# Output projection of a hybrid decoder block: 512 moving columns, left half along k, right half from ya's tiles, another last chain, stores on two queues

## The chip, the core and the metric

The kernel runs on one core of one Trainium2 chip. TensorE (PE) does matmuls into PSUM and loads its stationary operand separately (PEld); VectorE (DVE) and ScalarE (ACT) do elementwise work and are the two that read PSUM here; GpSimd (POOL) works on SBUF alone; SyncE (SP) issues DMAs. Every engine takes its instructions in order, and engines wait for each other by semaphores. The metric is the device time of one execution in microseconds; lower is better. The time shown for the kernel before is the median of 3 runs.

## What is computed

One layer of a decoder block with two parallel branches, an mLSTM (matrix memory) and a native sparse attention, over 512 tokens of width 1024 in float32. What matters here is how the layer ends:

```python
ya = jax.nn.sigmoid(p["m_o"]) * mh * jax.nn.silu(p["m_z"])
...
yb = yn * jax.nn.silu(p["n_z"])
merged = (jax.nn.sigmoid(p["g_a"]) * (ya @ w_branch_a[l])
          + jax.nn.sigmoid(p["g_b"]) * (yb @ w_branch_b[l]))
x = x + merged @ w_out[l]
...
return _rmsnorm(x, final_norm_g)
```

`_rmsnorm` multiplies each row by the inverse root of the mean of its squares plus 1e-6, and by a gain per column. `merged` is 512 x 1024, `w_out` 1024 x 1024.

## The kernel before

**Precision.** Every large product is done in three passes. Each float32 operand is split into a high part (rounded to the type that TensorE takes at full rate, float32r) and a low part, the rest; the product is high x high + high x low + low x high, all three summed in one PSUM bank. `split` (line 129) makes the two: ACT copies the raw tile to the high tile, VectorE subtracts the high from the raw to get the low. `mm3` (line 156) runs the three passes over a list of k blocks of 128 rows; the order is a·c, a·d, b·c with a, b the stationary high and low and c, d the moving ones. `passes` (line 199) is the same as a generator, for work that is fed in small steps.

**Weights.** `weights` (line 140) loads a raw tile of 128 x 1024 values (512 KB) on SP's queue into one of three buffers `wr`, and splits it into `wh` and `wl`, of which there are three each. A raw buffer is free once VectorE has subtracted; a high or low buffer once TensorE has read it for the last time. `wwide` (line 152) makes two such calls, for k blocks 0 to 3 and 4 to 7 of 256 columns.

**Order.** The Python text issues the work in one order; the framework places each engine's instructions by its own estimate of when they can run, and ACT and VectorE keep the order so placed. So a split may stand ahead of work that the text issued earlier. A stream (line 164) runs the projections and the branch products two loads ahead.

**The stages before the change.** The last jobs of the stream are, for j = 0 to 7 (`branch`, line 1030): 128 columns of the gates, of ya @ w_branch_a (24 matmuls of 512 moving columns on `yah` and `yal`, the split ya, [128, 8, 512] each) and of yb @ w_branch_b (12 matmuls on `ybh` and `ybl`). VectorE combines the two with the gates in tiles `s`, and the sum is split into `meh[:, j]` and `mel[:, j]`: merged, transposed, with its 1024 columns as 8 blocks of 128 partitions and the 512 tokens in the free dimension. After the stream, SP's queue loads x into `xo` [128, 4, 1024] and the gain into `fg`, and ACT loads the table that has Ln and Exp.

**The output projection (line 1088 on).** Four column groups `cc` of 256. Each loads its weights by `wwide` and runs over the four row blocks `tb` of 128 tokens: 24 matmuls with `meh` / `mel` stationary and 256 weight columns moving, into one of three banks `pp`. Behind each such block, VectorE adds half of the bank to x (the factor of the gates' sigmoid, which is done by tanh, leaves a 2), ACT squares the result with a running sum into `fs[:, tb, cc]`, and VectorE multiplies by the gain, in place. After the third group VectorE adds up the first three sums of squares and makes `fb` = sum/1024 + eps of them.

**The last chain (`scale_out`, line 1071).** When the fourth sum of a row block is there, ACT does Ln and Exp for a first value r of the inverse root (`fr`), VectorE forms v = last sum/1024 + `fb` (`fv`) and improves r by one Newton step (r·v·r, then 1.5 - half of it, times r). Then VectorE scales columns 0 to 511 and ACT 512 to 1023, and SP issues one store of 256 KB for each half.

Of the kernel before, what the change touches and what calls it, by code (L numbers as in the profile page):

```python
# [11 lines left out]
F32 = mybir.dt.float32  # L12
F32R = mybir.dt.float32r
I32 = mybir.dt.int32
AF = mybir.ActivationFunctionType
OP = mybir.AluOpType
AX = mybir.AxisListType.X

T = 512
D = 1024  # L20
NT = T // 128
ND = D // 128
EPS = 1e-6
# [40 lines left out]
def build(  # L64
# [4 lines left out]
    nc = tc.nc  # L69
# [17 lines left out]
    pe, pool = nc.tensor, nc.gpsimd  # L87
    act, dve = Engine(nc.scalar, "act"), Engine(nc.vector, "dve")
    A = act.activation

    pers = ctx.enter_context(tc.tile_pool(name="pers", bufs=1))
    wp = ctx.enter_context(tc.tile_pool(name="wp", bufs=2))
    psum = ctx.enter_context(tc.tile_pool(name="psum", bufs=2, space=bass.MemoryType.PSUM))

    def bank(tag, bufs):
        return psum.tile([128, 512], F32, name=tag, tag=tag, bufs=bufs)

    PP = lambda: bank("pp", 3)
    PS = lambda: bank("ps", 2)
    PT = lambda: bank("pt", 2)  # L100
    PO = lambda: bank("po", 1)

    def f(ap):
        return ap.bitcast(F32)
# [11 lines left out]
    mhalf = pers.tile([128, 4], F32, name="mhalf")  # L116
    pool.memset(mhalf, -0.5)

    def rsqrt(pl, v, n, tag):
        r = pl.tile([128, n], F32, name=tag + "r", tag=tag + "r")  # L120
        t = pl.tile([128, n], F32, name=tag + "t", tag=tag + "t")
        pool.tensor_tensor(r, v, mhalf[:, :n], OP.pow)
        dve.tensor_tensor(t, v, r, OP.mult)
        dve.tensor_tensor(t, t, r, OP.mult)
        dve.tensor_scalar(t, t, -0.5, 1.5, OP.mult, OP.add)
        dve.tensor_tensor(r, r, t, OP.mult)
        return r

    def split(src, hi, lo, eng="a"):
        if eng == "a":  # L130
            A(hi, src, AF.Copy)
        elif eng == "p":
            pool.tensor_scalar(hi, src, 1.0, 1.0, OP.mult, OP.mult)
        else:
            dve.tensor_copy(hi, src)
        dve.tensor_tensor(lo, src, f(hi), OP.subtract)
# [3 lines left out]
    def weights(src, eng="a"):  # L140
        nk, n = src.shape[1], src.shape[2]
        raw = wp.tile([128, nk, n], F32, name="wr", tag="wr", bufs=3)
        nc.sync.dma_start(raw, src)
        hi = wp.tile([128, nk, n], F32R, name="wh", tag="wh", bufs=3)
        lo = wp.tile([128, nk, n], F32R, name="wl", tag="wl", bufs=3)
        split(raw, hi, lo, eng)
        return hi, lo
# [4 lines left out]
    def wwide(view, c0):  # L152
        ws = [weights(view[:, k : k + 4, c0 : c0 + 256]) for k in (0, 4)]
        return (lambda k: ws[k // 4][0][:, k % 4, :]), (lambda k: ws[k // 4][1][:, k % 4, :])

    def mm3(ps, lh, ll, rh, rl, ks, start=True, stop=True):
        n = len(ks)
        for i, k in enumerate(ks):
            a, b, c, d = lh(k), ll(k), rh(k), rl(k)
            pe.matmul(ps, a, c, start=start and i == 0, stop=False)  # L160
            pe.matmul(ps, a, d, start=False, stop=False)  # L161
            pe.matmul(ps, b, c, start=False, stop=stop and i == n - 1)  # L162
# [86 lines left out]
    with tc.tile_pool(name="ph0", bufs=2, side="right") as p0, tc.tile_pool(  # L249
        name="small", bufs=1, side="right"  # L250
# [3 lines left out]
        raw = sp.tile([128, ND, SW], F32, name="sraw")  # L254
# [6 lines left out]
        for k in (0, 4):  # L261
            ks = slice(k, k + 4)
# [10 lines left out]
        for hf in range(2):  # L273
            ps = PS()
# [68 lines left out]
        last = None  # L343
        for tb in range(NT):
            ts = slice(tb * 128, (tb + 1) * 128)
            for hf in range(2):
                ks = slice(hf * 4, hf * 4 + 4)
# [9 lines left out]
            last = PP()  # L357
# [13 lines left out]
        rows = sp.tile([11, D], F32, name="rows")  # L371
# [11 lines left out]
        ps = PT()  # L383
# [25 lines left out]
        c1 = np.float32(6.28125)  # L409
# [265 lines left out]
    for src, dst in ((cpad, Ct), (spad, St)):  # L675
        ps = PT()
# [205 lines left out]
    yah = yap.tile([128, ND, T], F32R, name="yah")  # L882
    yal = yap.tile([128, ND, T], F32R, name="yal")
# [58 lines left out]
    for h in range(4):  # L942
# [11 lines left out]
        for sb in range(NT):  # L954
            o, n = KOFF[sb], 512 - sb * 128
            bias = cs[:, sb, h : h + 1]
# [5 lines left out]
        for sb in range(NT):  # L962
            o, n = KOFF[sb], 512 - sb * 128
# [33 lines left out]
        r = rsqrt(mp, va, NT, "rl")  # L997
# [26 lines left out]
    with tc.tile_pool(name="fin", bufs=1) as fp:  # L1024
        meh = fp.tile([128, ND, T], F32R, name="meh")
        mel = fp.tile([128, ND, T], F32R, name="mel")
        wav = w_branch_a[0].rearrange("(k p) c -> p k c", p=128)
        wbv = w_branch_b[0].rearrange("(k p) c -> p k c", p=128)
        wov = w_out[0].rearrange("(k p) c -> p k c", p=128)
        def branch(base, j, yh, yl, nk):  # L1030
            def gen(w):
                o = 0 if nk == ND else (j % 2) * 128
                ps = PP()
                yield from passes(
                    ps, lambda k: w[0][:, k, o : o + 128], lambda k: w[1][:, k, o : o + 128],
                    lambda k: yh[:, k], lambda k: yl[:, k], nk,
                )
                s = halves[base, j]
                dve.scalar_tensor_tensor(s, s, 1.0, ps, OP.add, OP.mult)
                if base == GB:  # L1040
                    t = halves.pop((GA, j))
                    dve.tensor_tensor(t, t, halves.pop((GB, j)), OP.add)
                    split(t, meh[:, j], mel[:, j])

            def load():
                if nk == ND:
                    return weights(wav[:, :, j * 128 : j * 128 + 128])
                if j % 2 == 0:
                    halves["w"] = weights(wbv[:, :, j * 128 : j * 128 + 256])
                return halves["w"]  # L1050

            stream.add(load, gen)

        for j in range(ND):
            for base in (GA, GB):
                if (base, j) in later[3:]:
                    gate_ab(base, j, sgp)
            branch(GA, j, yah, yal, ND)
            branch(GB, j, ybh, ybl, 4)
        stream.drain()  # L1060
        xo = fp.tile([128, NT, D], F32, name="xo")
        nc.sync.dma_start(xo, x[0].rearrange("(b p) c -> p b c", p=128))
        fg = fp.tile([128, D], F32, name="fg")
        nc.sync.dma_start(fg, final_norm_g.partition_broadcast(128))
        tc.keep_in_program_order(act.preload_act_table_set("natural_log_exp_and_others"))
        fs = fp.tile([128, NT, 4], F32, name="fs")
        fb = fp.tile([128, NT], F32, name="fb")
        fv = fp.tile([128, NT], F32, name="fv")
        fr = fp.tile([128, NT], F32, name="fr")

        def scale_out(tb):
            part, v, r = fb[:, tb : tb + 1], fv[:, tb : tb + 1], fr[:, tb : tb + 1]
            last = fs[:, tb, 3:4]
            A(r, last, AF.Ln, bias=part, scale=1.0 / D)
            dve.scalar_tensor_tensor(v, last, 1.0 / D, part, OP.mult, OP.add)
            A(r, r, AF.Exp, scale=-0.5)
            dve.scalar_tensor_tensor(v, r, v, r, OP.mult, OP.mult)
            dve.tensor_scalar(v, v, -0.5, 1.5, OP.mult, OP.add)
            dve.tensor_tensor(r, r, v, OP.mult)
            for hf in range(2):  # L1080
                hs = slice(hf * 512, hf * 512 + 512)
                if hf:
                    A(xo[:, tb, hs], xo[:, tb, hs], AF.Copy, scale=r)
                else:
                    dve.tensor_scalar(xo[:, tb, hs], xo[:, tb, hs], r, None, OP.mult)
                nc.sync.dma_start(out[0, tb * 128 : (tb + 1) * 128, hs], xo[:, tb, hs])

        for cc in range(4):
            wh, wl = wwide(wov, cc * 256)
            cs_ = slice(cc * 256, cc * 256 + 256)  # L1090
            for tb in range(NT):
                ps = PP()
                ts = slice(tb * 128, tb * 128 + 128)
                mm3(
                    ps[:, :256], lambda k: meh[:, k, ts], lambda k: mel[:, k, ts],
                    wh, wl, range(ND),
                )
                xv = xo[:, tb, cs_]
                dve.scalar_tensor_tensor(xv, ps[:, :256], 0.5, xv, OP.mult, OP.add)
                jk = fp.tile([128, 256], F32, name="jk", tag="jk", bufs=2)  # L1100
                A(jk, xv, AF.Square, accum_out=fs[:, tb, cc : cc + 1])
                dve.tensor_tensor(xv, xv, fg[:, cs_], OP.mult)
                if cc == 2:
                    v = fb[:, tb : tb + 1]
                    dve.tensor_reduce(v, fs[:, tb, 0:3], AX, OP.add)
                    dve.tensor_scalar(v, v, 1.0 / D, EPS, OP.mult, OP.add)
                if cc == 3:
                    scale_out(tb)


_INS = (
# [19 lines left out]
```

## Time and profile before

| | us |
|---|---|
| median of 3 runs | 645.48 (644.75 to 646.33) |
| the profiled execution, its own time | 644.24 |
| its span, first to last instruction | 642.4 |
| w_out stage: first matmul to last VectorE read of a bank | 589.55 to 635.97 |
| last matmul's read to the end of the span | 635.97 to 642.4 |

The granted clock of TensorE was 0.998 of full speed over the span. Times inside the span count from its first instruction. In a row of the timeline stand the start, the duration, the engine, the line (L80 is the wrapper through which all ACT and VectorE instructions are recorded, so these are told apart by their tiles), the operation, and output <- inputs with partitions x elements; in square brackets the engine's idle time before it and what ended it. A matmul's duration (0.28 or 0.39) includes its way through the array, and they overlap; the distance between their starts is the pitch. SPq is SP's DMA queue: its rows are the issues, not the transfers.

The costliest groups of the whole span, of which the w_out stage has the last three of TensorE:

```profile
L202 PE MATMUL pp<-hTh,wh 128*128 128x512 f32 (+1 forms) x488 | 192.2, 394 | 0.0
...
L161 PE MATMUL pp<-wl,meh 128*128 128x256 f32 x128 | 36.2, 283 | 0.0
L160 PE MATMUL pp<-wh,meh 128*128 128x256 f32 x128 | 36.2, 283 | 0.0
L162 PE MATMUL pp<-wh,mel 128*128 128x256 f32 x128 | 36.2, 284 | 0.0
```

### The profile page before, as it was taken

Reading aid. Unit: us, or ns where it says so; the run is one execution under the profiler, and the core shown is the slowest. Engines: PE = TensorE matmul, PEld = TensorE weight load, DVE = VectorE, ACT = ScalarE, POOL = GpSimd, SP = SyncE. Lnnn points to the kernel's source line nnn. Section 1 sums busy time; section 2 is a strip of 40 time slices with the busy share of each in tenths; the row PEclk is TensorE's granted clock in tenths of the full one; section 3 lists DMA queues with packets and bytes.
Section 4 is the critical chain, followed back from the end, with each engine's and each line's share of the span. In section 5 each row is a group of like instructions: output and inputs, shape, how many; then the busy total and the mean of one; then the engine's idle time right before and its main releaser. Section 6 shows DMA issues by size and latency. Waiting matters only on the chain.

```text
span 642.4 us, 9274 instructions
## 1 busy us (share of the span) xinstructions
PE 626.9 (98%) x3470; PEld 538.8 (84%) x3470; DVE 411.5 (64%) x878; ACT 302.4 (47%) x604; POOL 54.0 (8%) x114
## 2 busy tenths in 40 slices
PE   6999999999999999999999999999999999999995
PEld 4988788888878788888989889889888888888995
DVE  5796768767866865557669788696554233334455
ACT  5653554655655655435545546545322222223234
POOL 5000021121121231100000000000000000000000
PEclk9999999999999999999999999999999999999999
DMA  8476421122122212223313222232274242423203
GB/s 248 136 193 154 120 66 45 55 67 67 36 64 66 65 49 83 66 70 96 99 37 96 80 73 78 67 78 87 66 232 128 66 131 67 128 70 108 90 1 131
DMA packets 90124, 58.74 MB, mean 91 GB/s; under 512 B 4016, under 2 KB 86100, under 8 KB 90080
## 3 DMA queue, kind: packets, MB, share of 16 engines
q1 hardware_dynamic: 90080, 58.16, 31.8%
q8 instruction: 27, 0.44, 0.3%
q14 instruction: 17, 0.14, 0.1%
HBM read 55.01 MB, written 2.10 MB: 89 GB/s over the span
## 4 chain that ended last, share of the span: by engine, by line
PE 88%; DVE 7%; ACT 2%; DMA 1%; issue 1%; SPq 0%; POOL 0%; DVEq 0%; POOLq 0%
PE pp L204 21%; PE pp L202 21%; PE pp L206 21%; PE pp L162 3%; PE pp L160 3%; PE pp L161 3%; PE pt L784 2%; DVE wl L80 2%; PE po L797 1%; PE ps L769 1%; PE po L796 1%; PE ps L537 1%; ACT wh L80 1%; PE ps L770 1%; PE ps L162 1%
## 5 line engine op out<-in xcount | busy, mean ns | idle before, releaser
L202 PE MATMUL pp<-hTh,wh 128*128 128x512 f32 (+1 forms) x488 | 192.2, 394 | 0.0
L204 PE MATMUL pp<-hTl,wh 128*128 128x512 f32 (+1 forms) x488 | 191.3, 392 | 0.0
L206 PE MATMUL pp<-hTh,wl 128*128 128x512 f32 (+1 forms) x488 | 191.1, 392 | 0.0
L80 DVE TENSOR_TENSOR wl<-wr,wh 128x1024 fp32r<-128x1024 f32 x88 | 109.0, 1240 | 74.3 <-ACT wh L80 73.9
L80 ACT ACTIVATE wh<-wr 128x1024 fp32r<-128x1024 f32 x88 | 92.9, 1057 | 114.3 <-PE pp L204 82.8
L206 PEld LDWEIGHTS pp<-hTh,wl 128*128 128x128 f32 x488 | 91.8, 188 | 16.2
L202 PEld LDWEIGHTS pp<-hTh,wh 128*128 128x128 f32 x488 | 92.0, 188 | 15.3
L204 PEld LDWEIGHTS pp<-hTl,wh 128*128 128x128 f32 x488 | 92.0, 189 | 15.1
L778 POOL TENSOR_SCALAR P<-P,st 128x128 f32<-128x128 f32 (+1 forms) x64 | 38.5, 620 | 182.2 <-DVE st L80 134.1
L80 ACT ACTIVATE P<-P,st 128x128 f32<-128x128 f32 (+3 forms) x64 | 35.7, 558 | 36.6 <-DVE st L80 36.4
L80 DVE CUSTOM_DVE_ANT_0 P<-ps,cst 128x128 f32<-128x128 f32 (+3 forms) x64 | 30.4, 486 | 22.0 <-PE ps L770 21.6
L80 ACT ACTIVATE pth<-pt 128x512 fp32r<-128x512 f32 (+1 forms) x64 | 27.2, 434 | 29.8 <-PE pt L784 18.6
L80 DVE TENSOR_TENSOR ptl<-pt,pth 128x512 fp32r<-128x512 f32 (+1 forms) x64 | 30.4, 484 | 16.4 <-ACT pth L80 15.7
L204 PE MATMUL pp<-wl,hTh 128*128 128x256 f32 x128 | 36.2, 283 | 0.0
L206 PE MATMUL pp<-wh,hTl 128*128 128x256 f32 x128 | 36.2, 283 | 0.0
L202 PE MATMUL pp<-wh,hTh 128*128 128x256 f32 x128 | 36.2, 283 | 0.0
L161 PE MATMUL pp<-wl,meh 128*128 128x256 f32 x128 | 36.2, 283 | 0.0
L160 PE MATMUL pp<-wh,meh 128*128 128x256 f32 x128 | 36.2, 283 | 0.0
L162 PE MATMUL pp<-wh,mel 128*128 128x256 f32 x128 | 36.2, 284 | 0.0
L80 DVE SCALAR_TENSOR_TENSOR u<-pp,prm,u 128x511 f32<-128x511 f32 (+2 forms) x48 | 35.6, 742 | 0.4
L80 DVE SCALAR_TENSOR_TENSOR s<-s,pp 128x512 f32<-128x512 f32 x16 | 11.0, 687 | 29.5 <-PE pp L206 29.5
L784 PE MATMUL pt<-cst,P 128*128 128x128 f32 x160 | 28.6, 274 | 0.3 <-DVE ptl L80 0.3
(272 smaller groups left out, 1112.0 us busy)
## 6 DMA issues: line engine op xcount, KB each, us to landing
wr<-w_in SPq DMA_DIRECT2D x68, 512.0 KB, 3.9
wr<-w_branch_a SPq DMA_DIRECT2D x8, 512.0 KB, 3.8
wr<-w_out SPq DMA_DIRECT2D x8, 512.0 KB, 3.5
wr<-w_branch_b SPq DMA_DIRECT2D x4, 512.0 KB, 3.6
xo<-x SPq DMA_DIRECT2D x1, 2048.0 KB
out<-xo SPq DMA_DIRECT2D x8, 256.0 KB, 2.2
xt<-x SPq DMA_DIRECT2D x3, 512.0 KB, 5.8
k<-k SPq DMA_DIRECT2D x8, 128.0 KB, 2.3
```

The source lines that it names most:

```text
L80: ins = fn(*args, **kw)
L160: pe.matmul(ps, a, c, start=start and i == 0, stop=False)
L161: pe.matmul(ps, a, d, start=False, stop=False)
L162: pe.matmul(ps, b, c, start=False, stop=stop and i == n - 1)
L202: pe.matmul(ps, a, c, start=k == 0, stop=False)
L204: pe.matmul(ps, a, d, start=False, stop=False)
L206: pe.matmul(ps, b, c, start=False, stop=k == nk - 1)
L537: pe.matmul(ph[:, :64], W1[i][:, j, :], Xs[i][:, j].rearrange("p g n -> p (g n)"), start=j == 0, stop=j == 15,)
L769: pe.matmul(pss[:, :n], tq, kh[:, b, :n], start=True, stop=False)
L770: pe.matmul(pss[:, :n], tq, kl[:, b, :n], start=False, stop=True)
L778: pool.tensor_scalar(pj, pj, st[:, 2, j : j + 1], 1.0, OP.mult, OP.mult)
L784: pe.transpose(pt[:, (qb - kb) * 128 : (qb - kb) * 128 + 128], P[:, POFF[qb] + kb * 128 : POFF[qb] + kb * 128 + 128], ident,)
```

## The change

**Left half.** The columns 0 to 511 of the output are computed along k: four banks (two of `ps`, two of `pt`, which the stages before use and this one did not), one for each row block, stay open while four weight pairs of two k blocks and 512 columns each go by. A pair serves 4 x 6 matmuls of 512 moving columns.

**Right half.** The raw weights of columns 512 to 1023 are loaded in between, two k blocks at a time, on SP's queue into the same three `wr` buffers, and split into `yah` and `yal`, which branch A has read by then. There they stay, so each row block runs its 24 matmuls at once, 512 columns wide into a `pp` bank; the last row block is cut into two pieces of 256 columns.

**Pieces.** `piece` does the addition, the square and the gain on 512 columns at a time (256 for the last two). For the very last one the addition goes to a tile of its own, `xg`, so that the gain's product and ACT's Square both read it. `partial` makes `fb` from the sums so far, one after the left half for row blocks 0 to 2, two for the last.

**Last chain.** v comes first, the first value r = v to the power -0.5 is made on GpSimd (`mhalf` holds -0.5; GpSimd's other such power is in `rsqrt`, line 119), and the Newton step is the same. VectorE scales 640 columns and ACT 384. SP's queue stores the 640, ACT's queue the 384.

On the engines, TensorE has 168 matmuls of 512 and 48 of 256 columns in the stage. SP issues eight weight loads as before, in the order left, right, left, right, then four stores of 320 KB; ACT issues four stores of 192 KB. On ACT, the splits of pairs 0 to 2 and of the first three raw tiles stand ahead of the last `meh` split and the table load, pair 3 and the fourth raw tile behind them; VectorE's order is alike. In the third row block VectorE's scaling comes behind the addition of the last block's first piece, and ACT's store of it behind that piece's Square.

```diff
+        xg = fp.tile([128, 256], F32, name="xg")
+
+        def piece(tb, ps, c0, slot, own=None):
+            n = ps.shape[1]
+            xr = xo[:, tb, c0 : c0 + n]
+            xv = xr if own is None else own
+            dve.scalar_tensor_tensor(xv, ps, 0.5, xr, OP.mult, OP.add)
+            jk = fp.tile([128, 512], F32, name="jk", tag="jk", bufs=2)
+            A(jk[:, :n], xv, AF.Square, accum_out=fs[:, tb, slot : slot + 1])
+            dve.tensor_tensor(xr, xv, fg[:, c0 : c0 + n], OP.mult)
+
+        def partial(tb, slots):
+            v = fb[:, tb : tb + 1]
+            if slots == 1:
+                dve.tensor_scalar(v, fs[:, tb, 0:1], 1.0 / D, EPS, OP.mult, OP.add)
+            else:
+                dve.tensor_reduce(v, fs[:, tb, 0:slots], AX, OP.add)
+                dve.tensor_scalar(v, v, 1.0 / D, EPS, OP.mult, OP.add)
+
-        def scale_out(tb):
+        def scale_out(tb, slot):
             part, v, r = fb[:, tb : tb + 1], fv[:, tb : tb + 1], fr[:, tb : tb + 1]
-            last = fs[:, tb, 3:4]
-            A(r, last, AF.Ln, bias=part, scale=1.0 / D)
+            rows = slice(tb * 128, tb * 128 + 128)
+            last = fs[:, tb, slot : slot + 1]
             dve.scalar_tensor_tensor(v, last, 1.0 / D, part, OP.mult, OP.add)
-            A(r, r, AF.Exp, scale=-0.5)
+            pool.tensor_tensor(r, v, mhalf[:, 0:1], OP.pow)
             dve.scalar_tensor_tensor(v, r, v, r, OP.mult, OP.mult)
             dve.tensor_scalar(v, v, -0.5, 1.5, OP.mult, OP.add)
             dve.tensor_tensor(r, r, v, OP.mult)
-            for hf in range(2):
...
+            dve.tensor_scalar(xo[:, tb, 0:640], xo[:, tb, 0:640], r, None, OP.mult)
+            nc.sync.dma_start(out[0, rows, 0:640], xo[:, tb, 0:640])
+            A(xo[:, tb, 640:D], xo[:, tb, 640:D], AF.Copy, scale=r)
+            nc.scalar.dma_start(out[0, rows, 640:D], xo[:, tb, 640:D])
+
+        ts = [slice(tb * 128, tb * 128 + 128) for tb in range(NT)]
+
+        banks = [PS(), PT(), PS(), PT()]
+        for q in range(4):
+            wh, wl = weights(wov[:, 2 * q : 2 * q + 2, 0:512])
+            for tb in range(NT):
+                mm3(
+                    banks[tb], lambda k: meh[:, k, ts[tb]], lambda k: mel[:, k, ts[tb]],
+                    lambda k: wh[:, k - 2 * q], lambda k: wl[:, k - 2 * q],
+                    (2 * q, 2 * q + 1), start=q == 0, stop=q == 3,
+                )
+            ks = slice(2 * q, 2 * q + 2)
+            raw = wp.tile([128, 2, 512], F32, name="wr", tag="wr", bufs=3)
+            nc.sync.dma_start(raw, wov[:, ks, 512:D])
+            split(raw, yah[:, ks], yal[:, ks])
+
+        for tb in range(NT):
+            piece(tb, banks[tb], 0, 0)
+            if tb < 3:
+                partial(tb, 1)
+        for tb in range(NT):
+            cuts = (512, D) if tb < 3 else (512, 768, D)
+            for i, (c0, c1) in enumerate(zip(cuts, cuts[1:])):
+                ps = PP()
+                rs_ = slice(c0 - 512, c1 - 512)
+                mm3(
+                    ps[:, : c1 - c0], lambda k: meh[:, k, ts[tb]], lambda k: mel[:, k, ts[tb]],
+                    lambda k: yah[:, k, rs_], lambda k: yal[:, k, rs_], range(ND),
+                )
+                if tb == 3 and i == 0:
+                    piece(tb, ps[:, :256], 512, 1)
+                    partial(tb, 2)
+                elif tb == 3:
+                    piece(tb, ps[:, :256], 768, 2, xg)
+                    scale_out(tb, 2)
                 else:
-                    dve.tensor_scalar(xo[:, tb, hs], xo[:, tb, hs], r, None, OP.mult)
...
+                    piece(tb, ps, 512, 1)
+                    scale_out(tb, 1)
```

More of the change, by code (lines that the diff above doesn't have):

```diff
@@ L1079, in scale_out @@
             dve.tensor_tensor(r, r, v, OP.mult)
-            for hf in range(2):
-                hs = slice(hf * 512, hf * 512 + 512)
-                if hf:
-                    A(xo[:, tb, hs], xo[:, tb, hs], AF.Copy, scale=r)
-                else:
-                    dve.tensor_scalar(xo[:, tb, hs], xo[:, tb, hs], r, None, OP.mult)
[L1086 to L1108, printed above, removed]
```

## The prediction

> **What bounds the kernel now.** I read the page first: the engines' shares, the slices, the shares of the chain that ended last. The span is the profiled execution's own.
>
> ```profile
> span 642.4 us, 9274 instructions
> ...
> PE 626.9 (98%) x3470; PEld 538.8 (84%) x3470; DVE 411.5 (64%) x878; ACT 302.4 (47%) x604; POOL 54.0 (8%) x114
> ...
> PE   6999999999999999999999999999999999999995
> ...
> PE 88%; DVE 7%; ACT 2%; DMA 1%; issue 1%; SPq 0%; POOL 0%; DVEq 0%; POOLq 0%
> ```
>
> TensorE is busy in every slice but the first and the last, so in the stage that changes (w_out, the end of the span) two things set the time: how many matmuls follow each other at what pitch, and what is left when the last one is done. The timeline of TensorE gives the pitch of both widths, just before the stage and inside it (start, duration, engine, line, operands):
>
> ```profile
> 581.39 0.39 PE L202 MATMUL pp<-yah,wh 128*128 128x512 f32 x1
> 581.62 0.39 PE L204 MATMUL pp<-yal,wh 128*128 128x512 f32 x1
> ...
> 589.55 0.28 PE L160 MATMUL pp<-wh,meh 128*128 128x256 f32 x1
> 589.66 0.28 PE L161 MATMUL pp<-wl,meh 128*128 128x256 f32 x1
> 589.78 0.28 PE L162 MATMUL pp<-wh,mel 128*128 128x256 f32 x1
> ...
> 592.96 0.51 PE L162 MATMUL pp<-wh,mel 128*128 128x256 f32 x2
> ...
> 635.66 0.28 PE L162 MATMUL pp<-wh,mel 128*128 128x256 f32 x1
> ```
>
> From 581.39 to 589.55 lie the 24 matmuls of the last branch A tile and the 12 of the last branch B tile: 8.16 / 36 = 0.2267 us for 512 columns. The 16 x 24 = 384 matmuls of w_out go at 0.120. Their first starts at 589.55 and the last would start 383 x 0.120 = 45.96 later, at 635.51; it starts at 635.66. The missing 0.15 us is the slip around 592.96, where the two matmuls on the last mel tile stand late.
>
> The rest of the span is the chain behind the last matmul, in the timeline of all engines:
>
> ```profile
> 635.97 0.42 DVE L80 SCALAR_TENSOR_TENSOR xo<-pp,xo 128x256 f32<-128x256 f32 x1
> 636.43 0.42 ACT L80 ACTIVATE jk<-xo 128x256 f32<-128x256 f32 x1 [0.36 <-DVE xo L80]
> 636.75 0.19 ACT L80 ACTIVATION_READ_ACCUMULATOR jk<-xo 128x1 f32 x1
> 636.97 0.43 DVE L80 TENSOR_TENSOR xo<-xo,fg 128x256 f32<-128x256 f32 x1 [0.57 <-ACT jk L80]
> 637.30 0.20 ACT L80 ACTIVATE fr<-fr 128x1 f32<-128x1 f32 x1
> 637.32 0.15 DVE L80 SCALAR_TENSOR_TENSOR fv<-fs,fb 128x1 f32<-128x1 f32 x1
> 637.58 0.22 DVE L80 SCALAR_TENSOR_TENSOR fv<-fr,fv 128x1 f32<-128x1 f32 x1
> 638.02 0.16 DVE L80 TENSOR_TENSOR fr<-fr,fv 128x1 f32<-128x1 f32 x1
> 638.22 0.72 ACT L80 ACTIVATE xo<-xo,fr 128x512 f32<-128x512 f32 x1 [0.71 <-DVE fr L80]
> 638.22 0.49 DVE L80 TENSOR_SCALAR xo<-xo,fr 128x512 f32<-128x512 f32 x1
> 638.73 0.81 SPq L1086 DMA_DIRECT2D out<-xo  x2
> ```
>
> The last matmul would hand over to the next at 635.78, and VectorE reads its bank 0.19 us later. The sum of squares is there at 636.94, fr (the inverse root) at 638.18, the first of the last two stores is issued at 638.73, and 3.67 us later the span is over.
>
> **TensorE's share of the change.** Of 384 matmuls of 256 columns, 168 of 512 (96 in the left half along k, 72 in the right half of the first three row blocks) and 48 of 256 (the two quarters of the last row block) are left: 168 x 0.2267 + 48 x 0.120 = 43.85 us, where now 384 x 0.120 + 0.15 = 46.23 pass. That is **-2.38 us**, if nothing new waits. The 0.15 in it goes because mel's last tile is read first in the fourth quarter of the left half, some 16 us after the stage begins. In these rows a matmul costs 13.3 ns more than its columns at 2.4 per ns (106.7 and 213.3), whatever its width, which is why wide ones save.
>
> The Trainium skill (TensorE: Matmul & The Clock Gate, "Back-to-back issue gap") puts that fixed part at about 2.5 ns for an isolated matmul. By it one matmul of 512 instead of two of 256 would save 2.5 ns, not 13.3, and the sum over 168 pairs would be -0.4 us in place of -2.2. This trace's two pitches, 0.120 and 0.2267, speak for the larger number, and the measurement is used.
>
> **Whether the left half is fed.** Each quarter of it needs a new hi/lo pair, and between the pairs the raw tiles of the right half are loaded and split into yah and yal. All eight loads share three raw buffers, in SP's queue, in the order left, right, left, right; ACT and VectorE take the splits in the same order, and they may only write yah after branch A's last matmul has read it. The rows are of SP's timeline, the page's list of DMA issues, ACT's timeline and VectorE's:
>
> ```profile
> 570.11 0.37 SPq L143 DMA_DIRECT2D wr<-w_out  x1
> 578.32 0.37 SPq L143 DMA_DIRECT2D wr<-w_out  x1
> 583.76 0.37 SPq L143 DMA_DIRECT2D wr<-w_out  x1
> ...
> wr<-w_out SPq DMA_DIRECT2D x8, 512.0 KB, 3.5
> ...
> 581.41 1.06 ACT L80 ACTIVATE wh<-wr 128x1024 fp32r<-128x1024 f32 x1 [3.89 <-issue]
> 591.20 0.63 ACT L80 ACTIVATE meh<-s 128x512 fp32r<-128x512 f32 x1 [0.61 <-DVE s L80]
> 591.85 1.28 ACT L80 ACT_TABLE_LOAD   x1
> ...
> 582.51 1.23 DVE L80 TENSOR_TENSOR wl<-wr,wh 128x1024 fp32r<-128x1024 f32 x1 [4.22 <-ACT wh L80]
> 587.03 0.69 DVE L80 SCALAR_TENSOR_TENSOR s<-s,pp 128x512 f32<-128x512 f32 x1 [3.30 <-PE pp L206]
> ```
>
> The loads keep their size and, for the first four, their times: the second, third and fourth are issued at 570.11, 578.32 and 583.76 as now (their buffers come free by the same splits) and land 3.5 later. Pair 0 is split at 581.41 and 582.51, as now. The first split into yah starts near 587.0, when branch A is through; with 1.06 on ACT and 1.23 on VectorE, and VectorE's sums of the last branch tiles (0.69 each) between them, I get: yal 0 done 589.5, pair 1 at 591.2, yal 1 at 592.4. Raw 2 is issued when yal 0 frees its buffer, lands 593.0, pair 2 is ready 595.5. The last meh split on ACT now stands behind yah 2, whose load is issued at 591.2 and lands at 594.8: meh at 596.7, table load until 598.0, mel 598.0. Raw 3 is issued at 592.4 and lands 595.9; its split queues behind meh and the table load, 598.0 to 599.1, and pair 3 is complete at 600.5. TensorE asks for pairs 1, 2, 3 at 589.55 plus 5.44, 10.88, 16.32: 595.0, 600.4, 605.9. The covers are 3.8, 4.9 and 5.4 us. yal 3 follows near 602 and is wanted at 611.3. So VectorE and ACT, 64% and 47% busy, hide all of it: **0**.
>
> **The chain at the end.** Gone from it: Ln and Exp on ACT (0.6 us between the sum of squares and VectorE's 637.58, mostly). New in it: VectorE's v must be there first, then a power on GpSimd, of one column. The trace has that power on four columns, and a plain operation on one:
>
> ```profile
> L122 POOL TENSOR_TENSOR rlr<-va,mhalf 128x4 f32<-128x4 f32 x4 | 4.1, 1013 | 45.8 <-DVE va L80 45.8
> ...
> L307 POOL TENSOR_TENSOR r<-r,v 128x1 f32<-128x1 f32 x3 | 0.6, 190 | 0.2
> ...
> 332.30 0.17 DVE L80 TENSOR_SCALAR va<-va 128x4 f32<-128x4 f32 x1
> 332.55 1.03 POOL L122 TENSOR_TENSOR rlr<-va,mhalf 128x4 f32<-128x4 f32 x1 [1.59 <-DVE va L80]
> 333.61 0.16 DVE L80 TENSOR_TENSOR rlt<-va,rlr 128x4 f32<-128x4 f32 x1 [1.15 <-POOL rlr L122]
> ```
>
> The hops are 0.08 us to GpSimd and 0.03 back. One column costs between 0.40 (190 ns, plus a quarter of the 823 ns that four columns cost above it) and 1.01 (if the cost is the instruction's). The row is of the same operation but four times as wide, so I take the middle, 0.70. From the sum of squares to fr: 0.03 + 0.15 (v) + 0.08 + 0.70 + 0.03 + 0.60 (637.58 to 638.18, unchanged) = 1.59, now 1.24. The chain named shorter is **+0.35 us** longer (+0.05 to +0.66). The product with fg, now from a tile of its own (xg), runs beside ACT's Square; it takes nothing off, because v at 637.32 waits for fr today anyway.
>
> On this price the Trainium skill (GPSIMD Engine Reference, "Elementwise — side-by-side cycle accounting") counts some 2.6 cycles per element on top of a dispatch cost. Were the power like that, three columns fewer would save nothing, and the power would stay at 1.01, as in the row; the sum would then be 0.3 us less of a gain. The row alone can't tell the two apart.
>
> Scaling: 640 columns on VectorE, 384 on ACT. 0.49 x 640 / 512 = 0.61, 0.72 x 384 / 512 = 0.54; the first store leaves 0.65 after fr instead of 0.55: **+0.10**. The two stores then start together instead of 0.44 apart (0.81 less one issue of 0.37). Does that help? The windows of the last stores (PE, PEld, DVE, ACT, POOL busy, clock, DMA share, GB/s):
>
> ```profile
> 639.60:639.80 0.20, 0.00 (x0) 0.00 (x0) 0.00 (x0) 0.00 (x0) 0.00 (x0) 1.00 0.96 358
> 640.60:640.80 0.20, 0.00 (x0) 0.00 (x0) 0.00 (x0) 0.00 (x0) 0.00 (x0) 0.50 0.96 369
> 641.00:641.20 0.20, 0.00 (x0) 0.00 (x0) 0.00 (x0) 0.00 (x0) 0.00 (x0) 0.50 0.02 0
> ```
>
> All 16 DMA engines are full from 639.6 to 641: 512 KB at about 370 GB/s. The bytes are the limit, not the issue, so two queues give **0**. No DMA is issued by ACT in this trace; I bound that from -0.44 (the whole offset) to +0.37 (an issue that costs twice SP's).
>
> Nearer waits: VectorE now stands at GpSimd's power in each row block, with the next block's first read behind it. For blocks 0 to 2 the next bank is due 5.4 us later. For the last block it is due 2.9 us after the third's: there the chain 0.69 + 0.8 + 0.69 + 0.15 + 0.11 + 0.70 + 0.60 keeps VectorE until about 631.5, the bank is ready at 630.7, and with scaling, Square and product of that piece VectorE is free at 633.4, the last bank at 633.6. Cover 0.2; with a power of 1.01 it is gone and costs 0.2. ACT's third store stands ahead of the last Square, due at 634.0, and has a microsecond.
>
> **Sum.** -2.38 + 0.35 + 0.10 = -1.93 us. The profiled execution took 644.24 around its span of 642.4, so it would be 642.3 with a span of 640.5. The median of the runs shown, 645.48, lies 1.24 above it; less 1.93 that is **643.6**. With the bounds (power 0.40: -0.31; 1.01: +0.31 and +0.2; stores -0.44 to +0.37) the change lies between -2.7 and -1.05, the time between 642.8 and 644.4, and a median of three adds about 0.4 (the runs span 1.6).
>
> **Rivals.**
> The width gains nothing: with meh as the loaded operand and 512 moving columns the pitch is 2 x 0.120 = 0.240. For it: no row has this pair of operands at this width. Against: the fixed 13.3 ns stands in both rows. Only the 0.15 of the slip is saved then: -0.15 + 0.45 = +0.3, 645.8, no change that can be measured. The page's 2.5 ns, named above, would come out close to this, at 645.4.
>
> Slower: the left half starves. Place: pair 3, behind two loads that wait for buffers, behind meh and the table load on ACT. TensorE wants it at 605.9 and I have it at 600.5. From 5.4 us of delay it begins to cost, from 7.3 us (5.4 + 1.93) the change loses. For it: the order on ACT puts a load's landing ahead of meh, one late load holds everything behind it on three queues. Against: a landing of 3.5 would have to become 9, since both loads wait in parallel for most of it. At 10 us late: 645.48 - 1.93 + 4.6 = 648.2.
>
> **How the numbers follow.** Forecast 0.82, width gains nothing 0.08, starved 0.10. I call 0.3% (1.94 us) what a measurement of this kernel can tell from no change; my centre lies on it. Within the forecast the power decides the side: below 0.7 faster, above it not. By the shape of the other GpSimd rows (a cost per column) I lean to the cheaper side: 0.50 faster, 0.32 within. Same: 0.32 + 0.08 = 0.40; slower 0.10. The range is the forecast's with its noise, a little widened towards the first rival: 642.5 to 645.2; what it leaves out is under 0.2.
>
> **What would show it.** In the new trace: 0.2267 between the matmuls on meh with 512 columns; no gap over 0.1 us at the four quarters; the last VectorE read of a bank at about 633.6; a one-column power between 0.4 and 1.0; fr 1.6 us after the sum of squares; both last stores issued within 0.1 us and DMA full for 1.4 us. A pitch of 0.24, a wait of a first matmul on wl, or a store of ACT's that lands late would make the prediction wrong.

## The result, and the profile after

| | before | changed |
|---|---|---|
| median of the runs, us | 644.87 (5 runs, 644.51 to 646.33) | 642.91 (5 runs, 642.54 to 643.25) |
| ratio, 95% interval | | 0.9963 (0.9952 to 0.9973) |
| profiled execution: time / span, us | 644.24 / 642.4 | 642.91 / 641.1 |
| first w_out matmul to VectorE's last read of a bank | 46.42 | 44.03 |
| last read to the end of the span | 6.46 | 6.73 |

The kernel is 1.96 us faster by the medians, which is 0.30% of 644.87; the ratio in the table, taken over all runs, puts it at 0.37%, and its interval leaves out no change. The predicted time was 643.6 in a range of 642.5 to 645.2, so the time lies inside. But the named time is 0.29% below 645.48 (the sum, -1.93 us, is 0.299%), just on the near side of the 0.3%, or 1.94 us, that the prediction called what a measurement can tell from no change, and the measured change is beyond it.

The page of the changed kernel, the span and the engines' shares:

```profile
span 641.1 us, 8887 instructions
...
PE 624.7 (97%) x3302; PEld 529.9 (83%) x3302; DVE 408.7 (64%) x861; ACT 297.6 (46%) x582; POOL 56.2 (9%) x118
```

TensorE has 168 matmuls less and stays the bound. Where the stage begins, its timeline (start, duration, engine, line, operands):

```profile
590.13 0.39 PE L206 MATMUL pp<-ybh,wl 128*128 128x512 f32 x1
590.36 0.39 PE L160 MATMUL ps<-wh,meh 128*128 128x512 f32 x1
590.59 0.39 PE L161 MATMUL ps<-wl,meh 128*128 128x512 f32 x1
590.81 0.39 PE L162 MATMUL ps<-wh,mel 128*128 128x512 f32 x1
```

The pitch doesn't change where the branch product ends and w_out begins: 0.2267 with meh loaded, as with the weights loaded. The stage begins 0.81 later than in the profile of before (590.36, 589.55), although TensorE's work ahead of it was not changed. So spans of single profiles aren't compared below; stages are, from their first matmul on.

The end, in the timeline of all engines:

```profile
634.39 0.42 DVE L80 SCALAR_TENSOR_TENSOR xg<-pp,xo 128x256 f32<-128x256 f32 x1 [0.49 <-PE pp L162]
634.85 0.42 ACT L80 ACTIVATE jk<-xg 128x256 f32<-128x256 f32 x1 [1.66 <-DVE xg L80]
635.17 0.19 ACT L80 ACTIVATION_READ_ACCUMULATOR jk<-xg 128x1 f32 x1
635.39 0.16 DVE L80 SCALAR_TENSOR_TENSOR fv<-fs,fb 128x1 f32<-128x1 f32 x1
635.63 0.55 POOL L1094 TENSOR_TENSOR fr<-fv,mhalf 128x1 f32<-128x1 f32 x1 [4.12 <-DVE fv L80]
636.21 0.22 DVE L80 SCALAR_TENSOR_TENSOR fv<-fr,fv 128x1 f32<-128x1 f32 x1 [0.66 <-POOL fr L1094]
636.65 0.16 DVE L80 TENSOR_TENSOR fr<-fr,fv 128x1 f32<-128x1 f32 x1
636.84 0.62 ACT L80 ACTIVATE xo<-xo,fr 128x384 f32<-128x384 f32 x1 [1.49 <-DVE fr L80]
636.84 0.56 DVE L80 TENSOR_SCALAR xo<-xo,fr 128x640 f32<-128x640 f32 x1
637.42 0.33 SPq L1099 DMA_DIRECT2D out<-xo  x1
637.49 0.35 ACTq L1101 DMA_DIRECT2D out<-xo  x1
```

From the sum of squares (635.36) to fr (636.81) it takes 1.45, before 1.24. The reader sees VectorE idle for 0.66 until GpSimd's power is there. From fr to the first store it is 0.61, before 0.55. Both stores are issued within 0.07, and from the first one to the end it takes 3.70 (3.70 before).

### The profile page after: what moved, and what is told of

It reads as the page before. It is cut to its first block, busy times and chain, and to the rows that moved or that the text cites. A ratio compares the mean times of both kernels' runs of the same rounds, so it can differ in the third digit from the quotient of the medians.

```text
span 641.1 us, 8887 instructions
## 1 busy us (share of the span) xinstructions
PE 624.7 (97%) x3302; PEld 529.9 (83%) x3302; DVE 408.7 (64%) x861; ACT 297.6 (46%) x582; POOL 56.2 (9%) x118
## 4 chain that ended last, share of the span: by engine, by line
PE 87%; DVE 7%; ACT 2%; issue 2%; DMA 1%; SPq 0%; POOL 0%; POOLq 0%; DVEq 0%
PE pp L204 21%; PE pp L202 21%; PE pp L206 21%; PE pt L784 2%; DVE wl L80 2%; PE pp L162 2%; PE pp L160 2%; PE pp L161 2%; PE ps L162 1%; PE ps L160 1%; PE ps L161 1%; PE ps L769 1%; PE po L797 1%; ACT wh L80 1%; PE po L796 1%
## 5 line engine op out<-in xcount | busy, mean ns | idle before, releaser
L80 DVE TENSOR_TENSOR wl<-wr,wh 128x1024 fp32r<-128x1024 f32 x84 | 104.2, 1242 | 73.0 <-ACT wh L80 72.6
L80 ACT ACTIVATE wh<-wr 128x1024 fp32r<-128x1024 f32 x84 | 88.7, 1057 | 111.0 <-PE pp L204 80.2
L784 PEld LDWEIGHTS pt<-cst,P 128*128 128x128 f32 x160 | 20.7, 140 | 8.8 <-DVE ptl L80 2.2
L202 PE MATMUL pp<-yah,wh 128*128 128x512 f32 x64 | 25.0, 390 | 0.0
L206 PE MATMUL pp<-yah,wl 128*128 128x512 f32 x64 | 24.9, 389 | 0.0
```

Of the source, the lines that this page charges most:

```text
L80: ins = fn(*args, **kw)
L202: pe.matmul(ps, a, c, start=k == 0, stop=False)
L206: pe.matmul(ps, b, c, start=False, stop=k == nk - 1)
L784: pe.transpose(pt[:, (qb - kb) * 128 : (qb - kb) * 128 + 128], P[:, POFF[qb] + kb * 128 : POFF[qb] + kb * 128 + 128], ident,)
```

## The experiments

Of each run two lengths are compared, taken from its own trace: the first w_out matmul to the last read of a bank (the row of the last addition, xg or xo <- pp), and that read to the end of the span. Their sum is called the stage. Where the table says one run, only the trace is compared, not the time.

| run | to last read | behind it | stage | median, ratio (interval) |
|---|---|---|---|---|
| before | 46.42 | 6.46 | 52.88 | |
| changed | 44.03 | 6.73 | 50.76 | 642.91, 0.9963 (0.9952 to 0.9973) |
| changed, again | 44.03 | 6.73 | 50.76 | 643.02, 0.9966 (0.9955 to 0.9977) |
| widths alone | 44.03 | 6.45 | 50.48 | 642.60, 0.9967 (0.9955 to 0.9980) |
| last chain alone | 47.98 | 6.84 | 54.82 | 646.72, 1.0030 (1.0019 to 1.0042) |
| last chain alone, Ln and Exp | 46.41 | 6.49 | 52.90 | 645.00, 0.9999 (0.9990 to 1.0008) |
| changed, Ln and Exp | 44.03 | 6.47 | 50.50 | 643.13, 0.9967 (0.9955 to 0.9980) |
| changed, one store queue | 44.03 | 6.82 | 50.85 | one run |
| changed, last block uncut | 43.72 | 7.23 | 50.95 | one run |
| changed, cut 384 + 128 | 45.09 | 6.51 | 51.60 | one run |
| changed, four last stores | 44.03 | 6.89 | 50.92 | one run |
| changed, more powers | 44.03 | 6.73 | 50.76 | one run |
| changed, twelve loads | 44.02 | 6.78 | 50.80 | one run |
| changed, folded scaling | 44.03 | 6.37 | 50.40 | 641.99, 0.9957 (0.9944 to 0.9970) |

**The changed kernel again.**

> The changed kernel once more, beside its parts on one chip. Measure of all runs here: the length from the first w_out matmul to the end of the span (52.88 us before, 50.76 after) and its pieces. The theory (the width gives -2.4, the last chain gives 0.25 back) expects 50.7 to 50.9 again wherever the stage begins, and a ratio near 0.997. Rival (part of the gain comes from ahead of the stage, since its start moved from 589.55 to 590.36 between the two profiles): the start of the stage would be as late again, and the ratio differ.

The stage began at 590.48 and took 50.76 again, to the hundredth. In the fourteen profiles it began between 589.55 and 591.39, and the spread is there early: GpSimd's first memset of a tile X begins at 41.0 to 42.7 in the same profiles, and the distance from it to the stage is the same to within 0.5 (41.1 before, 41.6 changed). So most of the spread arises in the first 42 us, long ahead of the changed code, and a single profile's span carries it. A shift of a few tenths ahead of the stage is not ruled out by this, but the medians (-1.96 in the first comparison, -2.13 in the second) leave little room for one beside the stage's -2.12.

**The widths alone.** In the changed kernel, the last chain of before:

```diff
+            A(r, last, AF.Ln, bias=part, scale=1.0 / D)
             dve.scalar_tensor_tensor(v, last, 1.0 / D, part, OP.mult, OP.add)
-            pool.tensor_tensor(r, v, mhalf[:, 0:1], OP.pow)
+            A(r, r, AF.Exp, scale=-0.5)
...
-            dve.tensor_scalar(xo[:, tb, 0:640], xo[:, tb, 0:640], r, None, OP.mult)
+            dve.tensor_scalar(xo[:, tb, 0:512], xo[:, tb, 0:512], r, None, OP.mult)
...
-                    piece(tb, ps[:, :256], 768, 2, xg)
+                    piece(tb, ps[:, :256], 768, 2)
```

> The widths and the k order of the change, with the last chain of before (Ln and Exp on ACT, 512 and 512 columns scaled, both stores on SP's queue, no tile xg). Theory: from the first matmul to the last read of a bank 44.0 as in the changed kernel, behind it 6.46 as before, together 50.5, that is 0.25 shorter than the changed kernel and 2.4 shorter than before; time 2.2 to 2.4 below before. Rival (the shorter chain is a part of the gain): longer than the changed kernel, 51 or more.

44.03 and 6.45: the whole gain of the change is in the widths and the order along k, 2.40 of stage, and the new chain gives 0.28 of it back. The theory holds. This kernel has both the widths and the order, but the starts of the matmuls tell them apart: in the changed kernel no two starts of the stage lie more than 0.227 apart, so the slip of 0.15 around 592.96 is gone with the order, and 168 x (0.240 - 0.2267) = 2.24 is the width's part.

**The last chain alone.** The loops of before, with the power, xg, 640 and 384 columns and two queues:

```diff
-            A(r, last, AF.Ln, bias=part, scale=1.0 / D)
             dve.scalar_tensor_tensor(v, last, 1.0 / D, part, OP.mult, OP.add)
-            A(r, r, AF.Exp, scale=-0.5)
+            pool.tensor_tensor(r, v, mhalf[:, 0:1], OP.pow)
...
+                xr = xo[:, tb, cs_]
+                xv = xg if cc == 3 and tb == 3 else xr
+                dve.scalar_tensor_tensor(xv, ps[:, :256], 0.5, xr, OP.mult, OP.add)
```

> The kernel before with the last chain of the change alone (power on GpSimd, xg for the last piece, 640 and 384 columns, two queues); 384 matmuls of 256 columns stay. Theory: 46.4 to the last read, then 6.7 as in the changed kernel: 53.1, 0.25 longer than before; time the same to 0.4 longer. Rival (the chain is shorter): 52.5 or less.

The chain is no gain, but the size was a miss: 54.82 for 53.1. The last read, not the part behind it, came 1.56 late. VectorE's timeline of this kernel in the last group, two row blocks:

```profile
631.25 0.42 DVE L80 SCALAR_TENSOR_TENSOR xo<-pp,xo 128x256 f32<-128x256 f32 x1
632.39 0.43 DVE L80 TENSOR_TENSOR xo<-xo,fg 128x256 f32<-128x256 f32 x1 [0.72 <-ACT jk L80]
632.73 0.15 DVE L80 SCALAR_TENSOR_TENSOR fv<-fs,fb 128x1 f32<-128x1 f32 x1
633.55 0.22 DVE L80 SCALAR_TENSOR_TENSOR fv<-fr,fv 128x1 f32<-128x1 f32 x1 [0.67 <-POOL fr L1077]
...
634.66 0.42 DVE L80 SCALAR_TENSOR_TENSOR xo<-pp,xo 128x256 f32<-128x256 f32 x1
```

One block takes VectorE 3.41 with its two waits, for ACT's Square and for GpSimd, while a block of 24 narrow matmuls takes TensorE 2.88. The reads show no wait for TensorE any more: VectorE has become the bound of the group. In the changed kernel a block of 24 wide matmuls takes 5.44, and the same chain fits; even at the last bank, 2.88 behind the one ahead of it, VectorE has waited for TensorE for 0.49 (the first row of the end shown above).

**The last chain with Ln and Exp in it.** To tell the wait for GpSimd from the wider scaling, the kernel just shown with the power taken back out:

```diff
-            pool.tensor_tensor(r, v, mhalf[:, 0:1], OP.pow)
+            A(r, last, AF.Ln, bias=part, scale=1.0 / D)
+            A(r, r, AF.Exp, scale=-0.5)
```

> The kernel before with the new scaling and stores and xg, but Ln and Exp instead of the power. With the power, row blocks of 256 columns, 2.88 apart, had VectorE busy or waiting for 3.4 per block, and the last read came 1.56 late. Theory (it was the wait for GpSimd): without it VectorE keeps up, 46.4 to 46.6 to the last read, 6.47 behind it, 52.9 to 53.1. Rival (it was the wider scaling, 640 for 512): again above 47.5 to the last read.

46.41 and 6.49: VectorE keeps up although it still scales 640 columns, so it was the wait for GpSimd. With Ln and Exp the rest of the new chain is worth nothing either way (52.90 against 52.88, ratio 0.9999).

**Ln and Exp in the changed kernel.** The same edit there:

> The changed kernel with Ln and Exp on ACT in place of the power on GpSimd; two queues, 640 and 384 columns and xg stay. Theory: the sum of squares to fr takes 1.24 as before, not 1.45, so the stage is 0.2 shorter than the changed kernel, 50.55; time 0.1 to 0.3 below it, within what repeated runs scatter. Rival (the power's hops are hidden by the product with fg, so nothing is gained by Ln and Exp): 1.45 again.

From 1.45 to 1.20, the stage 50.50. The time can't show a quarter of a microsecond (643.13), the trace can.

**What a power costs.** Seven more in the changed kernel, of which nothing is used:

```diff
+        for n in (1, 2, 4, 8, 16, 32, 64):
+            pool.tensor_tensor(po_[:, :n], pw[:, :n], ph[:, :n], OP.pow)
```

> The changed kernel with seven further powers on GpSimd, of 1, 2, 4, 8, 16, 32 and 64 columns on tiles of their own, nothing of it used (two memsets go with it). Theory (a fixed cost and a cost per column, from 0.55 at one column and 1.01 at four): 0.55, 0.70, 1.01, 1.63, 2.9, 5.3, 10.2. Rival (the cost is the instruction's, with some other cause for 0.55): flat near 1.0 up to 16 columns. If GpSimd runs them in the left half, the stage is as long as in the changed kernel, 50.7 to 50.9.

They ran near 470, when GpSimd had nothing else. The groups of that kernel on GpSimd, by shape (busy us, mean ns of one):

```profile
L1125 POOL TENSOR_TENSOR pw_out<-pw,ph 128x64 f32<-128x64 f32 x1 | 10.6, 10552 | 0.1
...
L1125 POOL TENSOR_TENSOR pw_out<-pw,ph 128x8 f32<-128x8 f32 x1 | 1.6, 1637 | 0.1
...
L1125 POOL TENSOR_TENSOR pw_out<-pw,ph 128x4 f32<-128x4 f32 x1 | 1.0, 1007 | 0.1
L1125 POOL TENSOR_TENSOR pw_out<-pw,ph 128x2 f32<-128x2 f32 x1 | 0.7, 706 | 0.1
L1125 POOL TENSOR_TENSOR pw_out<-pw,ph 128x1 f32<-128x1 f32 x1 | 0.5, 548 | 0.1
```

From one column to 64 it is (10552 - 548) / 63 = 159 ns per column, on 390 ns that every power pays. The cost is the columns', as the theory had it.

**One queue for the stores.**

```diff
-            nc.scalar.dma_start(out[0, rows, 640:D], xo[:, tb, 640:D])
+            nc.sync.dma_start(out[0, rows, 640:D], xo[:, tb, 640:D])
```

> The changed kernel with all stores on SP's queue. Theory (the last 512 KB are limited by the DMA engines, so the second queue saves nothing): the second store is issued 0.4 later, the end comes 4.31 after fr as in the changed kernel, 4.2 to 4.45. Rival (the second queue saves the offset of the issues): 4.6 to 4.75.

SP's timeline, the two issues, with fr at 637.90 and the end of the span at 642.24:

```profile
638.51 0.33 SPq L1099 DMA_DIRECT2D out<-xo  x1
638.94 0.38 SPq L1101 DMA_DIRECT2D out<-xo  x1
```

The second store leaves 0.43 behind the first, and the end comes 4.34 after fr, with two queues 4.31: the second queue is worth 0.03. (The stage is 0.09 longer, of which 0.06 lies ahead of fr, most of it in the start of the Square.)

**Four last stores.** The last row block's scaling and stores in halves (320 and 320, 192 and 192):

```diff
+            n = 2 if tb == 3 else 1
+            for p in range(n):
+                a, b = p * 640 // n, (p + 1) * 640 // n
+                dve.tensor_scalar(xo[:, tb, a:b], xo[:, tb, a:b], r, None, OP.mult)
+                nc.sync.dma_start(out[0, rows, a:b], xo[:, tb, a:b])
...
```

> The last row block's scaling and stores in four pieces (320 and 320 on VectorE and SP, 192 and 192 on ACT and ACT's queue). Theory (the data are limited by the DMA engines from the first issue on): the first issue comes about 0.35 after fr instead of 0.61, and the end 0.2 to 0.25 earlier, 4.1 after fr, if the second pieces are issued before the first ones have gone. Rival (each store pays a fixed time, and the last issue decides): the last issue comes at 0.75 to 0.95 after fr, and the end is the same or up to 0.3 later.

The theory was wrong here. The issues in the timeline, with fr at 636.39:

```profile
636.91 0.82 ACTq L1105 DMA_DIRECT2D out<-xo  x2
636.84 0.81 SPq L1102 DMA_DIRECT2D out<-xo  x2
```

The first leaves 0.45 after fr instead of 0.61, but the end comes 4.47 after fr instead of 4.31. The rival had the number right (the same or up to 0.3 later), but its reason, the last issue, isn't the cause: the DMA engines are full without a gap, from 637.8 to 639.2, and the last issue starts at 637.3. Windows of 0.2 us of this kernel, two of the stretch in which they are full and the one in which it ends (share of the DMA engines and GB/s are the last two columns):

```profile
638.00:638.20 0.20, 0.00 (x0) 0.00 (x0) 0.00 (x0) 0.00 (x0) 0.00 (x0) 0.50 1.02 342
...
639.00:639.20 0.20, 0.00 (x0) 0.00 (x0) 0.00 (x0) 0.00 (x0) 0.00 (x0) 0.50 0.98 314
639.20:639.40 0.20, 0.00 (x0) 0.00 (x0) 0.00 (x0) 0.00 (x0) 0.00 (x0) 0.50 0.24 69
```

and of the changed kernel:

```profile
638.80:639.00 0.20, 0.00 (x0) 0.00 (x0) 0.00 (x0) 0.00 (x0) 0.00 (x0) 0.50 0.96 369
...
639.40:639.60 0.20, 0.00 (x0) 0.00 (x0) 0.00 (x0) 0.00 (x0) 0.00 (x0) 0.50 1.01 361
639.60:639.80 0.20, 0.00 (x0) 0.00 (x0) 0.00 (x0) 0.00 (x0) 0.00 (x0) 0.50 0.29 92
```

Full engines move some 330 GB/s in four stores of 1280 and 768 bytes a row, and some 370 in two of 2560 and 1536; whether the shorter rows or the greater number of stores makes the difference, no run here tells. The last bytes go some 2.85 after fr in both kernels (near 639.25 here, near 639.66 there, by the shares of the last windows), so the earlier start is eaten by the slower rate; then the end of the span takes 1.6 instead of 1.45. SP's semaphore records, which the views leave out, show behind the last landing two more waits here than in the changed kernel, 0.06 each, which would be 0.12 of that 0.15; no run was made to test it.

**The last block uncut.** One piece of 512 columns, 24 matmuls for 48 (`cuts = (512, D)` for all blocks, xg 512 wide):

> The changed kernel with the last row block uncut, 24 matmuls of 512 columns instead of 48 of 256. Theory (pitch 0.2267 against 0.120): first matmul to last read 44.03 - 0.32 = 43.7; behind it an addition of 0.69 for 0.42 and a Square of 0.63 for 0.42, so 6.73 + 0.48 = 7.2; together 50.9, 0.16 longer than the changed kernel. VectorE's last product (0.69) is done before the power, or delays v by up to 0.1. Rival (the pitch with meh as the loaded operand is not that of the branch stage): another length of the first part.

43.72 and 7.23, as expected to 0.03 on both sides: the cut costs TensorE 0.31 and saves 0.50 behind it.

**A narrower last piece.** `cuts = (512, 896, D)` for the last block:

> The last row block cut into 384 and 128 columns instead of 256 and 256. Theory (a matmul costs its columns at 2.4 per ns and 13.3 ns): pitches 0.1733 and 0.0667, the same sum, so 44.03 to the last read, or 0.1 to 0.2 later if VectorE is not free; the addition and the Square of 128 columns take 0.25 less together (VectorE 0.42 for 256 and 0.69 for 512), so 6.45 behind it, together 50.5. Rival (below 0.12 the pitch is set by loading the stationary operand): 24 matmuls of 128 at 0.12, the last read 1.3 later.

TensorE's timeline of this kernel, around the cut:

```profile
632.99 0.33 PE L161 MATMUL pp<-yal,meh 128*128 128x384 f32 x1
633.16 0.33 PE L162 MATMUL pp<-yah,mel 128*128 128x384 f32 x1
633.34 0.22 PE L160 MATMUL pp<-yah,meh 128*128 128x128 f32 x1
...
635.74 0.28 PE L161 MATMUL pp<-yal,meh 128*128 128x128 f32 x1
635.85 0.28 PE L162 MATMUL pp<-yah,mel 128*128 128x128 f32 x1
```

384 columns go at 0.173: 160 ns for the columns at 2.4 per ns, and the same 13.3 ns. 128 go at 0.111 and not at 0.067. The loads of the stationary operand in the same stretch (PEld):

```profile
633.34 0.19 PEld L161 LDWEIGHTS pp<-yal,meh 128*128 128x128 f32 x1
633.45 0.19 PEld L162 LDWEIGHTS pp<-yah,mel 128*128 128x128 f32 x1
633.56 0.19 PEld L160 LDWEIGHTS pp<-yah,meh 128*128 128x128 f32 x1
```

They start 0.111 apart as well, and each matmul of 128 columns starts some 0.06 behind its own load, so in this stretch the loads set the pace. The rival holds, with a floor of 0.111 for its 0.12: 1.06 lost in front, 0.22 gained behind.

**Twelve loads.** Each raw tile of the right half is loaded and split twice:

```diff
+            raw2 = wp.tile([128, 2, 512], F32, name="wr", tag="wr", bufs=3)
+            nc.sync.dma_start(raw2, wov[:, ks, 512:D])
+            split(raw2, yah[:, ks], yal[:, ks])
```

> The changed kernel with each raw tile of the right half loaded and split twice, so twelve loads of 512 KB through the three buffers instead of eight (the result is the same). In the changed kernel pair 3 is complete 9.0 after the first matmul and wanted at 16.3. Theory (the covers are real, 5 to 8 each): pair 3 comes 6 to 9 later, so the left half ends 0 to 2 later, and not more. Rival (the left half is fed without cover): the delay of each quarter adds up, 4 or more.

VectorE's low splits of pairs 2 and 3 in this kernel, whose first w_out matmul starts at 591.00:

```profile
598.22 1.23 DVE L80 TENSOR_TENSOR wl<-wr,wh 128x1024 fp32r<-128x1024 f32 x1 [1.30 <-ACT wh L80]
...
604.34 1.22 DVE L80 TENSOR_TENSOR wl<-wr,wh 128x1024 fp32r<-128x1024 f32 x1
```

Pair 3 is complete 14.6 after the first matmul, 5.6 later than in the changed kernel (a little under the 6 to 9 expected), and still 1.8 ahead of its use at 16.3. The stage is as long as without the extra loads. Four loads of 512 KB and their splits cost nothing: the cover is real.

**Folded scaling.** Ln and Exp, and the last product of the Newton step taken into the scaling (r times the factor v, in another order of rounding; ACT's scaling by r stands right behind Exp):

```diff
-            dve.tensor_tensor(r, r, v, OP.mult)
-            dve.tensor_scalar(xo[:, tb, 0:640], xo[:, tb, 0:640], r, None, OP.mult)
+            dve.tensor_scalar(xo[:, tb, 0:704], xo[:, tb, 0:704], r, v, OP.mult, OP.mult)
...
-            A(xo[:, tb, 640:D], xo[:, tb, 640:D], AF.Copy, scale=r)
+            A(xo[:, tb, 704:D], xo[:, tb, 704:D], AF.Copy, scale=r)
...
+            A(xo[:, tb, 704:D], xo[:, tb, 704:D], AF.Copy, scale=v)
```

> The changed kernel with Ln and Exp in place of the power and the last product of the Newton step folded into the scaling: VectorE multiplies 704 columns by both factors in one instruction, ACT multiplies its 320 by the first factor while VectorE makes the second, then by that. Theory: the sum of squares to the start of VectorE's scaling takes 1.05 to 1.1 instead of 1.48 (0.2 by Ln and Exp, 0.19 by the folding), the stage 50.25 to 50.4; time 0.3 to 0.5 below the changed kernel. Rival (ACT's two scalings in a row end later than one): the last store is issued as late as with Ln and Exp alone, stage 50.5.

The end of that kernel's timeline on both engines:

```profile
635.39 0.56 ACT L80 ACTIVATE xo<-xo,fr 128x320 f32<-128x320 f32 x1
...
635.83 0.65 DVE L80 TENSOR_SCALAR xo<-xo,fr,fv 128x704 f32<-128x704 f32 x1
635.98 0.56 ACT L80 ACTIVATE xo<-xo,fv 128x320 f32<-128x320 f32 x1
636.50 0.33 SPq L1100 DMA_DIRECT2D out<-xo  x1
```

From the sum of squares (634.80) to the scaling it takes 1.03, 0.20 less than with Ln and Exp alone (1.23); half of that goes to the wider scaling, 0.65 for 0.55. The stage is 50.40, the shortest of all, and the time 641.99. Its interval overlaps that of the changed kernel, so only the trace, by 0.36, puts it ahead.

## Why the prediction came out as it did

*TensorE's share, -2.38.* Measured 44.03 - 46.42 = -2.39. Of this, 2.24 is the width and 0.15 the slip that the new order leaves out. Both the pitch with meh loaded and the fixed 13.3 ns are as read from the two widths of the trace of before. The first rival (no gain by width) is out, 384 columns at 0.173 confirm the 13.3. The 2.5 ns of the Trainium skill (TensorE: Matmul & The Clock Gate, "Back-to-back issue gap"), given there for an isolated matmul, don't fit these pairs of load and matmul, and the measurement decides. The line does not go on downwards: at 128 columns there is a floor.

*The feeding of the left half, 0.* Right, and safer than told. The step "The first split into yah starts near 587.0, when branch A is through" was wrong: in the changed kernel

```profile
583.76 1.06 ACT L80 ACTIVATE yah<-wr 128x1024 fp32r<-128x1024 f32 x1
...
598.15 1.22 DVE L80 TENSOR_TENSOR wl<-wr,wh 128x1024 fp32r<-128x1024 f32 x1 [1.06 <-ACT wh L80]
```

the first split into yah (ACT's timeline) runs at 583.76, while branch A, 582.20 to 587.4, is still reading: it needs only k blocks 0 and 1, which branch A has read first. Pair 3 (VectorE's) is complete at 599.37, 9.0 after the first matmul, and the cover (how long it is ready before TensorE wants it) is 7.3 instead of 5.4. The second rival (starved) stayed away even with twelve loads.

*The chain at the end, +0.35.* This is the step that failed, in size and not in kind: it is +0.21. "I take the middle, 0.70" was the wrong choice between 0.40 and 1.01: the power took 0.55. The lower bound's way of reckoning, a fixed part and a part per column, was the right one. Its sizes were not: it took 190 ns, a plain operation's whole time, and 206 ns for the column, where a power has a fixed part of 390 ns and 159 ns per column; so one column lay 0.15 above that bound. The hops (0.08, 0.03) and the rest are as told. The 2.6 cycles per element of the Trainium skill (GPSIMD Engine Reference, "Elementwise — side-by-side cycle accounting"), which it gives for an addition, don't carry over to a power: here it is 159 ns per column.

*Scaling, +0.10.* Measured 0.61 - 0.55 = +0.06, for 0.56 on VectorE, not 0.61: scaling the whole 0.49 by 640 / 512 scaled the instruction's fixed part along with its columns. On ACT it went the other way, for the same reason: 384 columns took 0.62, not 0.54.

*Two queues, 0.* Right: 0.03. The reason given, that the DMA engines are full and not the issue late, holds for the four stores too, at a lower rate.

*The nearer waits.* The cover of 0.2 at the last bank was 0.49, of which the cheaper power explains 0.15; nothing was lost there.

*The sum, -1.93.* By the traces it is 50.76 - 52.88 = -2.12, 0.19 more than forecast: 0.14 of it the chain, 0.04 the scaling. The medians of the first comparison give -1.96, those of the second 645.15 - 643.02 = -2.13. So the mechanism and the signs were right, and the 0.15 by which the power was mis-sized put the forecast, -1.93, on the wrong side of the line at 1.94: with the measured power alone the sum is -2.08, or 0.32%. That the medians of the first comparison come within 0.03 of the forecast is luck, since the second gives 0.17 more. The centre lay on the line, as the prediction said, and the cheaper power that it leaned to in its chances was not the one in its sum. The named time also started from a median of 645.48; more runs of before gave 644.87 and 645.15. Of the 0.69 between 643.6 and 642.91 that is 0.61.

## What to carry to other kernels

Where TensorE is the bound and every matmul reloads its operand, read the pitch at two widths from the trace: what the pitch has beyond its columns is a price per instruction that wider moving operands save. That line held here from 256 to 512 columns; at 128 a floor took over. Change a chain at the end only after adding up its hops: a power on an idle engine can be slower than two table functions on the one that already has the data, and in a loop whose period is near the chain's it turns the engine that waits into the bound. Judge changes of a few tenths by a stage of the trace, counted from its own first instruction, when the start of the program alone scatters by more.

## What was not expected of the hardware

The start of one and the same stage scattered by 1.84 us between profiles (589.55 to 591.39), and an instruction near 42 us by 1.71 already. A matmul of 128 columns with its operand loaded anew cost 0.111, hardly less than one of 256 at 0.120. And the 16 DMA engines, full in both cases, moved 512 KB of stores at some 330 GB/s in four pieces and 370 in two.
